# Two attention merges on GpSimd, one maximum for two lists, and a row scaling two steps later

## The chip, the core and the metric

The kernel runs on one core of a Trainium2 chip. A core has a matrix engine (TensorE, PE in the profile, with its weight loads as PEld), a vector engine (VectorE, DVE), an engine for functions (ScalarE, ACT), a general engine (GpSimd, POOL) and a queue that issues transfers (SyncE, SP). Each engine works through its own list of instructions in order and waits on semaphores for the others. The metric is the device time of one execution in microseconds; three runs of the kernel before took 1610.02 to 1610.79 us, with a median of 1610.67.

## What is computed

One decoder block over 1024 tokens of width 1024. Attention runs in three dilation groups with 8 heads each; the groups are merged per head with weights that come from their softmax denominators. Beside it runs a gated causal convolution. Both are mixed, normalised by rows and added to the input, and a SwiGLU feed-forward network follows. Cut to what the change touches:

```python
for g, (window, dilation) in enumerate(DILATED_GROUPS):
    o_g, lse_g = dilated_group_attention(q[:, :, g], k[:, :, g], v[:, :, g], tab, window, dilation)
alpha = softmax(stack(lses), axis=0)               # weights of the three groups
o = einsum('gbsh,gbshd->bshd', alpha, stack(outs)) # the merge
y_attn = o.reshape(B, S, 512) @ w_attn_out
...
x = x + rms_norm(merged @ w_mix_out, g_post_mix)
h = rms_norm(x, g_pre_ffn)                         # the row scaling
x = x + rms_norm(swiglu_ffn(h, w_ffn_in, w_ffn_out), g_post_ffn)
```

## The kernel before

Nearly all products are made of three 16-bit products each: a number is split into a high and a low half precision part after a scaling by a power of two, and high times high, high times low and low times high are added up. The scalings need bounds of the numbers' sizes; `largest` (L176) makes such a bound of one or two parameter vectors: ScalarE squares each list of 8 numbers per partition (L182), VectorE adds the second list to the first where there are two (L186) and takes the maximum (L187). One call has two lists (L264, the scale and offset of the convolution's normalisation); it falls into the stage of the gates, where TensorE runs quarter products (L619 to L621), VectorE the convolution (L1003) and GpSimd the weights' subtractions (L458, L477 and others). L1103 adds two quarter results on VectorE, and a later product waits for it.

The order of the work is written out by hand. TensorE's instructions are issued in a fixed sequence, and after every three 512-column products (six 256-column ones) `tick` (L363) counts a step and lets background generators issue a piece of work on the other engines. A generator that yields n is left alone for n steps: `yield 1` moves what follows two steps down, `yield 3` four. `later(n, ...)` plans a piece n steps ahead. So the changes in the kernel are changes of the engine and of the position in the engines' lists; what runs when is then settled by the semaphores.

Attention (L1283) goes over twelve pairs of a group and a pair of heads, eight blocks of 128 queries each. Of each block TensorE makes the scores (L1355), VectorE adds the bias and takes a minimum (L1359), ScalarE takes exponentials (L1369), TensorE transposes (L1392), ScalarE and VectorE split the result (L1397, L1405), and TensorE multiplies by the values (L1421 to L1423). The transposes come three blocks after the scores and the values five. The score banks, the transpose banks and the output banks in PSUM are two each. For the next pair GpSimd copies keys and queries to the other half of the partitions (L1207, L1208) and scales the bias tile (L1212), a few blocks ahead. GpSimd's queue also issues the stores of values (L1247), of statistics and outputs (L1378).

A pair's merge (L1437) begins when the third group of a pair of heads is done. `hp` is the pair of heads, 0 to 3; those of 0 and 1 fall between 700 and 755 us, in the middle of attention, those of 2 and 3 at its end. It loads the first two groups' outputs (L1222), makes the weights of the groups in small instructions on VectorE (L1452 to L1461), multiplies the three outputs by them (L1465, 128x1024 each), adds them (L1467, L1470), has ScalarE sum the squares (L1473), and has TensorE transpose the result (L1487). The results of hp 0 and 1 are stored (L1502) and loaded again later (L1510).

After attention the mixing product runs over row tiles of 128 tokens, the first two together, then one by one (L1944, 48 products a tile). Behind each tile a generator (L1639) works on its rows: sums of squares on ScalarE (L1624), a row factor and the residual on VectorE (L1632, L1636), then the second normalisation: ScalarE's sum of squares (L1647), a root and five small VectorE instructions for the row factor (L1606), and ScalarE's scaling of the rows by it (L1649). After tiles 3 and 7 the four scaled tiles are transposed in eight groups (L1657), three steps apart after tile 3 and two after tile 7; each group takes one of two PSUM banks, which ScalarE empties (L1663) before it splits the group (L1531, with VectorE's L1532). ScalarE also splits weights in that stage (L448).

Of the kernel before, what the change touches and what calls it, by code (L numbers as in the profile page):

```python
# [14 lines left out]
AF = mybir.ActivationFunctionType  # L15
OP = mybir.AluOpType
AX = mybir.AxisListType
# [54 lines left out]
class Build:  # L72
# [103 lines left out]
    def largest(self, k, *cols, after=0):  # L176

        nc = self.nc
        q = [self.tiny(8, "pq", 4) for _ in cols]
        m = self.tiny(1, "pm", 4)  # L180
        for x, c in zip(q, cols):
            nc.scalar.activation(x, self.col8(c), AF.Square, scale=k)  # L182

        def most():
            if len(q) > 1:
                nc.vector.tensor_tensor(q[0], q[0], q[1], op=OP.add)  # L186
            nc.vector.tensor_reduce(m, q[0], AX.X, OP.max)  # L187

        if after:
            self.later(after, most)  # L190
        else:
            most()
        return m
# [1243 lines left out]
    def merge(self, hp, st, last):  # L1437


        nc = self.nc  # L1440

        late = 1 + (hp > 1)
        while hp > 1 and hp > len(self.OT) + 2:
            yield 0
        O = [*self.others(hp), last]
        last = None
        yield 1 + late
        t = self.tiny(96, "mrg", 2)
        m, r = (t[:, i * 16:(i + 1) * 16].rearrange("p (u e) -> p u e", u=8) for i in range(2))
        w = t[:, 48:].rearrange("p (g u e) -> p g u e", g=3, u=8)  # L1450
        low, tot = st[:, :, :, 0:2], st[:, :, :, 2:4]
        nc.vector.tensor_reduce(m, low.rearrange("p g u e -> p u e g"), AX.X, OP.min)  # L1452
        nc.vector.tensor_tensor(w, low, m.unsqueeze(1).to_broadcast([128, 3, 8, 2]), op=OP.subtract)
        nc.scalar.activation(t[:, 48:], t[:, 48:], AF.Exp, scale=-1.0)
        yield late
        nc.vector.tensor_tensor(tot, tot, w, op=OP.mult)
        nc.vector.tensor_reduce(m, tot.rearrange("p g u e -> p u e g"), AX.X, OP.add)
        nc.vector.reciprocal(r, m)
        x = t[:, 16:32]
        nc.vector.tensor_scalar(x, x, self.vun, None, op0=OP.mult)  # L1460
        nc.vector.tensor_tensor(w, w, r.unsqueeze(1).to_broadcast([128, 3, 8, 2]), op=OP.mult)  # L1461
        for g in range(3):
            y = O[g].rearrange("p (u h c) -> p u h c", u=8, h=2)
            a = w[:, g].unsqueeze(3).to_broadcast([128, 8, 2, 64])
            nc.vector.tensor_tensor(y, y, a, op=OP.mult)  # L1465
            yield late
        nc.vector.tensor_tensor(O[1], O[1], O[2], op=OP.add)  # L1467
        O[2] = y = a = None
        yield late
        nc.vector.tensor_tensor(O[0], O[0], O[1], op=OP.add)  # L1470
        O[1] = None
        yield 2
        nc.scalar.activation(self.junk, O[0], AF.Square, scale=self.o_scale, accum_out=self.osq[:, hp:hp + 1])  # L1473
        self.measured += 1
        if hp == 3:
            assert self.measured == 4
            self.mixing = self.bg(self.mix_scales())
        yield 1 + 2 * late
        if hp < 2:
            hi = self.slot()  # L1480
        else:
            hi, lo = self.two(T)
        for h in range(2):
            ps = self.bank("t")
            r = slice(h * 64, h * 64 + 64)
            for u in range(8):
                nc.tensor.transpose(ps.rearrange("p (m u) -> p u m", u=8)[:, u], O[0][r, u * 128:(u + 1) * 128],  # L1487
                                    self.ident[r, r])
            y = ps
            a = hi[:, h * H:(h + 1) * H]  # L1490
            if hp > 1:
                nc.scalar.activation(a, y, AF.Copy, scale=self.o_scale)
                nc.vector.scalar_tensor_tensor(lo[:, h * H:(h + 1) * H], y, self.o_scale, a,
                                               op0=OP.mult, op1=OP.subtract)
            else:
                nc.scalar.copy(a, y)
            ps = y = a = None
            yield late
        if hp > 1:
            self.OT[hp] = hi, lo  # L1500
        else:
            self.nc.gpsimd.dma_start(self.d_ot[hp], hi)  # L1502
# [136 lines left out]
    def mix_norm(self, tt, banks, x):  # L1639
        nc = self.nc  # L1640
        x2 = self.ring()
        yield from self.residual(banks, x, self.g_mix, x2)
        nc.sync.dma_start(self.d_x2[tt], x2)
        yield 1
        hn = self.slot()
        ss = self.tiny(4, "ss", 4)
        nc.scalar.activation(hn, x2, AF.Square, scale=ROOT, accum_out=ss[:, 0:1])  # L1647
        r = self.rstd_rows(ss[:, 0:1], self.eps_rms)
        nc.scalar.activation(hn, x2, AF.Copy, scale=r)  # L1649
        self.hn[tt // 4].append(hn)  # L1650
        if tt % 4 == 3:
            yield 14 if tt == 3 else 8
            op, y = [], None
            for kt in range(8):
                ps = self.bank("s")
                for i in range(4):
                    nc.tensor.transpose(ps[:, i * 128:(i + 1) * 128], self.hn[tt // 4][i][:, kt * 128:(kt + 1) * 128], self.ident)  # L1657
                if y is not None:
                    op.append(self.split(y, H, F16))
                if kt % 2 == 0:  # L1660
                    x = self.slot()
                y = x[:, (kt % 2) * H:(kt % 2 + 1) * H]
                nc.scalar.activation(y, ps, AF.Copy, scale=self.gain[1][:, kt:kt + 1])  # L1663
                self.h2f[tt // 4].append(y)
                yield 2 if tt == 3 else 1
            op.append(self.split(y, H, F16))
            self.h2[tt // 4] = op
            self.hn[tt // 4] = None
# [723 lines left out]
```

## Time and profile before

| | before |
|---|---|
| median of 3 runs | 1610.67 us |
| the profiled execution | 1611.6 us |
| its span, first to last instruction | 1609.7 us |
| mean granted clock of TensorE | 0.997 |
| ScalarE busy | 1084.6 us |
| GpSimd busy | 451.6 us |

The page of the profile shows how long each engine was busy; a list of waits shows which instruction waited for which; a list by stretches shows the busy time of PE, PEld, DVE, ACT and POOL in that order, each with its count of instructions, then the granted clock, the share of the transfer engines and GB/s. In lists in order of time the columns are the start, the duration, the engine, the line of the kernel, the operation, what it writes and reads, its shape and how many; in brackets the idle time before it and what ended it. Lists of one line's instructions give the shortest, median and longest duration in ns. Matmul records overlap: one of 512 columns is shown with 0.38 us, and the next starts 0.22 us after it. In the table's profiled execution the clock of TensorE was at half in two stretches of 3.41 us in the middle of the run and at the very end, and else full.

### The profile page before, as it was taken

The numbers are of one execution on the slowest core, as the hardware profiler recorded it, in microseconds if no ns is written. First come the engines' busy times: TensorE is split into PE (matmuls) and PEld (weight loads), VectorE is DVE, ScalarE is ACT, GpSimd is POOL, SyncE is SP. The second block draws the span as 40 slices with busy tenths as digits, with TensorE's granted clock in tenths as the row PEclk, the third lists the DMA queues.
The fourth block names the chain that finished last, engine by engine and source line by source line (L and its number), as shares of the span: only waits on it lengthen the run. The fifth ranks groups of instructions, "written<-read, shape, count | busy, mean of one in ns | idle before, by whom it ended". The sixth has DMA issues, their size and how long they took to land.

```text
span 1609.7 us, 25675 instructions
## 1 busy us (share of the span) xinstructions
PE 1582.1 (98%) x9085; PEld 849.2 (53%) x9085; DVE 1265.0 (79%) x2458; ACT 1084.6 (67%) x2069; POOL 451.6 (28%) x377
## 2 busy tenths in 40 slices
PE   8999999999999999999999999999999999999998
PEld 7744444444444789976654444444444444444443
DVE  6889999988888878887686765876666666777887
ACT  6476678777787569877654747767666666465654
POOL 0006777777777253663502200000000000000000
PEclk9999999999999999999999999999999999999999
DMA  4353355555566865677848332044444334494424
GB/s 176 109 200 115 113 208 184 194 190 187 161 174 167 249 190 156 166 222 205 246 179 322 153 107 103 27 170 151 150 167 148 125 125 144 144 384 134 156 92 164
DMA packets 164381, 271.87 MB, mean 169 GB/s; under 512 B 63921, under 2 KB 83052, under 8 KB 164252
## 3 DMA queue, kind: packets, MB, share of 16 engines
q1 hardware_dynamic: 160044, 258.06, 47.9%
q0 software_dynamic: 3920, 11.91, 2.5%
q8 instruction: 71, 1.16, 0.3%
q14 instruction: 58, 0.48, 0.1%
q10 hardware_dynamic: 288, 0.27, 0.0%
HBM read 196.35 MB, written 78.55 MB: 171 GB/s over the span
## 4 chain that ended last, share of the span: by engine, by line
PE 78%; DVE 12%; ACT 5%; issue 2%; DMA 2%; POOL 0%; SPq 0%; DVEq 0%; ACTq 0%; POOLq 0%
PE p L619 14%; PE p L620 14%; PE p L621 14%; PE p L2274 9%; PE p L603 4%; PE p L607 4%; PE p L605 4%; DVE p L1003 2%; PE p L857 2%; PE p L1260 2%; PE p L1262 2%; PE p L1264 2%; PE p L1392 2%; DVE b L449 2%; PE p L1355 2%
## 5 line engine op out<-in xcount | busy, mean ns | idle before, releaser
L621 PE MATMUL p<-b,b 128*128 128x512 f16 x1032 | 391.1, 379 | 1.4 <-POOL b L458 1.4
L620 PE MATMUL p<-b,b 128*128 128x512 f16 x1032 | 391.0, 379 | 0.0
L619 PE MATMUL p<-b,b 128*128 128x512 f16 x1032 | 391.0, 379 | 0.1
L2274 PE MATMUL p<-b 128*128 128x512 f16 x924 | 199.9, 379 | 0.6 <-DVE b L449 0.5
L621 PEld LDWEIGHTS <-b 128*128 128x128 f16 x1032 | 100.9, 98 | 124.6 <-POOL b L458 3.3
L619 PEld LDWEIGHTS <-b 128*128 128x128 f16 x1032 | 101.0, 98 | 121.0
L1003 DVE SCALAR_TENSOR_TENSOR p<-b,par,p 128x511 f32<-128x511 f32 (+14 forms) x232 | 164.1, 739 | 0.0
L620 PEld LDWEIGHTS <-b 128*128 128x128 f16 x1032 | 100.8, 98 | 116.8 <-issue 0.3
L2274 PEld LDWEIGHTS <-b 128*128 128x128 f16 x924 | 90.4, 98 | 110.0 <-issue 1.4
L603 PE MATMUL p<-b,b 128*128 128x512 f16 (+1 forms) x368 | 140.8, 383 | 1.6 <-ACT b L448 1.6
L607 PE MATMUL p<-b,b 128*128 128x512 f16 (+1 forms) x368 | 140.6, 382 | 0.4 <-DVE b L449 0.4
L605 PE MATMUL p<-b,b 128*128 128x512 f16 (+1 forms) x368 | 140.2, 381 | 0.0
L458 POOL TENSOR_TENSOR b<-d,b 128x1024 f16<-128x1024 f32 x44 | 93.9, 2133 | 89.9 <-ACT b L457 89.9
L449 DVE SCALAR_TENSOR_TENSOR b<-d,sc,b 128x1024 f16<-128x1024 f32 x40 | 51.3, 1282 | 85.9 <-ACT b L448 85.9
L1260 PE MATMUL p<-b,b 128*128 128x256 f16 x384 | 104.7, 273 | 0.1
L1264 PE MATMUL p<-b,b 128*128 128x256 f16 x384 | 104.7, 273 | 0.0
L1262 PE MATMUL p<-b,b 128*128 128x256 f16 x384 | 104.7, 273 | 0.0
L1369 ACT ACTIVATE c<-c,stat 128x128 f32<-128x128 f32 (+1 forms) x192 | 84.4, 444 | 6.2 <-DVE stat L1359 6.1
L1944 PE MATMUL p<-b,b 128*128 128x512 f16 x384 | 85.8, 383 | 0.0
L1359 DVE CUSTOM_DVE_ANT_0 c<-p,bt,sig 128x128 f32<-128x128 f32 (+1 forms) x192 | 70.7, 406 | 16.2 <-PE p L1355 11.6
L1003 DVE SCALAR_TENSOR_TENSOR p<-c,pairs,p 128x511 f32<-128x511 f32 (+6 forms) x112 | 82.7, 739 | 0.0
L449 DVE SCALAR_TENSOR_TENSOR b<-c,fs,b 128x512 f16<-128x512 f32 x77 | 57.4, 745 | 24.6 <-ACT b L448 24.5
(352 smaller groups left out, 3480.1 us busy)
## 6 DMA issues: line engine op xcount, KB each, us to landing
b<-w_in SPq DMA_DIRECT2D x30, 512.0 KB, 4.7
b<-w_v SPq DMA_DIRECT2D x24, 512.0 KB, 4.6
b<-w_fi SPq DMA_DIRECT2D x24, 512.0 KB, 6.2
d<-w_in SPq DMA_DIRECT2D x23, 512.0 KB, 4.2
dqS<-c SPq DMA_DIRECT2D x44, 256.0 KB, 2.2
b<-w_fo SPq DMA_DIRECT2D x22, 512.0 KB, 4.3
b<-w_fo SPq DMA_DIRECT2D x44, 256.0 KB, 5.4
c<-dqS SPq DMA_DIRECT2D x44, 256.0 KB, 4.1
```

The source lines that it names most:

```text
L449: self.nc.vector.scalar_tensor_tensor(lo, x, w, hi, op0=OP.mult, op1=OP.subtract)
L603: nc.tensor.matmul(ps, hi[:, s], a, start=kt == 0, stop=False)
L605: nc.tensor.matmul(ps, hi[:, s], b, start=False, stop=False)
L607: nc.tensor.matmul(ps, lo[:, s], a, start=False, stop=kt == nk - 1)
L619: nc.tensor.matmul(ps, hi[:, s], a, start=first and kt == 0, stop=False, skip_group_check=True)
L620: nc.tensor.matmul(ps, hi[:, s], b, start=False, stop=False, skip_group_check=True)
L621: nc.tensor.matmul(ps, lo[:, s], a, start=False, stop=kt == 3, skip_group_check=True)
L1003: nc.vector.scalar_tensor_tensor(A[i][:, j:], src[i][:, :H - j], w[i], A[i][:, j:], op0=OP.mult, op1=OP.add)
L1260: nc.tensor.matmul(o, a, hi[:, s], start=kt == 0, stop=False)
L1262: nc.tensor.matmul(o, a, lo[:, s], start=False, stop=False)
L1264: nc.tensor.matmul(o, b, hi[:, s], start=False, stop=kt == KT - 1)
L2274: nc.tensor.matmul(acc[t], x, y, start=first and e == 0, stop=last and e == 2, skip_group_check=True)
```

## The change

Three things are changed. `largest` puts the squares of its one or two lists side by side in one tile of 16 and takes a single maximum of all of them, instead of adding the lists first. In the merges of hp 0 and 1 the three products and two sums are issued to GpSimd instead of VectorE, with four steps between them instead of two, and six steps instead of three to the sum of squares; the merges of hp 2 and 3 stay on VectorE at their places. In `mix_norm` the scaling of the rows comes two steps after the row factor instead of in the same one.

```diff
     def largest(self, k, *cols, after=0):
...
-        q = [self.tiny(8, "pq", 4) for _ in cols]
+        q = self.tiny(16, "pq", 4)
         m = self.tiny(1, "pm", 4)
-        for x, c in zip(q, cols):
-            nc.scalar.activation(x, self.col8(c), AF.Square, scale=k)
+        for i, c in enumerate(cols):
+            nc.scalar.activation(q[:, 8 * i:8 * i + 8], self.col8(c), AF.Square, scale=k)
 
         def most():
-            if len(q) > 1:
-                nc.vector.tensor_tensor(q[0], q[0], q[1], op=OP.add)
-            nc.vector.tensor_reduce(m, q[0], AX.X, OP.max)
+            nc.vector.tensor_reduce(m, q[:, :8 * len(cols)], AX.X, OP.max)
...
         late = 1 + (hp > 1)
+        by, gap = (nc.gpsimd, 3) if hp < 2 else (nc.vector, late)
...
         for g in range(3):
             y = O[g].rearrange("p (u h c) -> p u h c", u=8, h=2)
             a = w[:, g].unsqueeze(3).to_broadcast([128, 8, 2, 64])
-            nc.vector.tensor_tensor(y, y, a, op=OP.mult)
-            yield late
-        nc.vector.tensor_tensor(O[1], O[1], O[2], op=OP.add)
+            by.tensor_tensor(y, y, a, op=OP.mult)
+            yield gap
+        by.tensor_tensor(O[1], O[1], O[2], op=OP.add)
         O[2] = y = a = None
-        yield late
-        nc.vector.tensor_tensor(O[0], O[0], O[1], op=OP.add)
+        yield gap
+        by.tensor_tensor(O[0], O[0], O[1], op=OP.add)
         O[1] = None
-        yield 2
+        yield 5 if hp < 2 else 2
         nc.scalar.activation(self.junk, O[0], AF.Square, scale=self.o_scale, accum_out=self.osq[:, hp:hp + 1])
...
         nc.scalar.activation(hn, x2, AF.Square, scale=ROOT, accum_out=ss[:, 0:1])
         r = self.rstd_rows(ss[:, 0:1], self.eps_rms)
+        yield 1
         nc.scalar.activation(hn, x2, AF.Copy, scale=r)
```

## The prediction

> **What bounds the kernel now.** I read the page first, then who TensorE waited for (over the whole run, then from 700 to 735 us), then the stretches around the longest waits with the granted clock.
>
> ```profile
> span 1609.7 us, 25675 instructions
> PE 1582.1 (98%) x9085; PEld 849.2 (53%) x9085; DVE 1265.0 (79%) x2458; ACT 1084.6 (67%) x2069; POOL 451.6 (28%) x377
> ...
> PE p L1657 <- ACT b L1663: 3.7, 2, 2.9
> PE p L619 <- DVE c L1103: 2.3, 1, 2.3
> ```
> ```profile
> PE p L1392 <- DVE c L1405: 0.8, 1, 0.8
> PE p L1487 <- DVE c L1405: 0.8, 1, 0.8
> PE p L1355 <- DVE stat L1359: 0.5, 2, 0.3
> ```
> ```profile
> 706.00:722.00 16.00, 14.66 (x143) 10.86 (x142) 15.50 (x40) 10.96 (x35) 5.00 (x7) 1.00 0.73 220
> 720.53:723.95 3.42, 1.91 (x16) 1.07 (x14) 3.14 (x10) 2.87 (x9) 2.57 (x4) 1.00 0.34 101
> 723.95:727.36 3.41, 3.36 (x20) 2.15 (x20) 3.24 (x11) 1.73 (x6) 0.00 (x0) 0.50 0.27 77
> ...
> 966.29:969.71 3.42, 1.11 (x7) 0.78 (x8) 1.87 (x3) 3.42 (x7) 0.00 (x0) 1.00 0.28 105
> 969.71:973.12 3.41, 3.41 (x11) 1.78 (x10) 2.34 (x5) 3.41 (x8) 0.00 (x0) 0.50 0.00 0
> ```
>
> TensorE sets the time: 1582 of 1610 us. Only stalls of TensorE can be won, and a relieved engine gains nothing by itself. Three stalls lie where the change has a part: one wait of 2.3 us (L619), a group of short ones between 706 and 727, and one of 2.9 us in the transposes of L1657. After the last two the clock stands at 0.50 for 3.41 us; each such stretch follows one in which TensorE was busy 1.91 or 1.11 of 3.42 us. The stages between these places run without waits, so what is won there should reach the end.
>
> **One maximum.** L186, the sum of two lists of 8 numbers, goes; L187 reduces 16 numbers instead of 8.
>
> ```profile
> 202.34 1.99 DVE L186 TENSOR_TENSOR pq<-pq,pq 128x8 f32<-128x8 f32 x1
> ...
> 205.72 0.15 DVE L187 TENSOR_REDUCE pm<-pq 128x1 f32<-128x8 f32 x1
> 205.79 0.73 DVE L1003 SCALAR_TENSOR_TENSOR p<-b,par,p 128x500 f32<-128x500 f32 x1
> ```
> ```profile
> 202.18 2.12 POOL L458 TENSOR_TENSOR b<-d,b 128x1024 f16<-128x1024 f32 x1 [1.11 <-ACT b L457]
> ...
> 205.61 1.27 POOL L478 TENSOR_TENSOR d<-d,d 128x512 f32<-128x512 f32 x1
> ```
> ```profile
> 204.54 0.38 PE L621 MATMUL p<-b,b 128*128 128x512 f16 x1
> 207.18 0.38 PE L619 MATMUL p<-b,c 128*128 128x512 f16 x1 [2.26 <-DVE c L1103]
> ```
>
> L186 took 1.99 us for 8 elements and ended with POOL's L458 (202.18 + 2.12): it stood still while POOL worked. The two instructions beside POOL's L478 did not: L187 reads one list, L1003 one operand from SBUF and one from PSUM. So VectorE is 2.0 us earlier at L1103, for which TensorE waits. TensorE starts a 512-column matmul every 0.22 us, so L619 would have begun at 204.76 and lost 2.4 us; 0.4 of it stays, **2.0 us go**.
>
> **The merges on GpSimd.** Per merge five VectorE instructions go; GpSimd gets them, the first product at the old step, each next one four steps later instead of two.
>
> ```profile
> L1465 DVE TENSOR_TENSOR b<-b,mrg x12: 1212/1218/1226, 706.2 to 839.6; 128x1024 f32<-128x1024 f32 x12
> L1025 POOL TENSOR_TENSOR b<-b,b x7: 2357/2367/2380, 226.8 to 530.0; 128x1024 f32<-128x1024 f32 x7
> L1212 POOL TENSOR_SCALAR bt<-bt,rsig x12: 1562/1563/2595, 570.4 to 802.9; 128x512 f32<-128x512 f32 x12
> ```
> ```profile
> 705.64 0.50 DVE L1461 TENSOR_TENSOR mrg<-mrg 128x48 f32<-128x48 f32 x1
> ...
> 728.77 0.35 DVE L1359 CUSTOM_DVE_ANT_0 c<-p,bt,sig 128x128 f32<-128x128 f32 x1 [0.99 <-issue]
> ```
> ```profile
> 703.46 0.61 POOL L1207 COPY b<-b 64x512 f16<-64x512 f16 x1
> ...
> 707.22 1.62 POOL L1212 TENSOR_SCALAR bt<-bt,rsig 128x512 f32<-128x512 f32 x1 [1.14 <-DMA bt<-rep]
> ```
> ```profile
> 719.02 1.15 ACT L1473 ACTIVATE junk<-b,cs 128x1024 bf16<-128x1024 f32 x1
> ```
>
> VectorE is freed of 5 x 1.22 = 6.1 us, once around 706 to 717 and once around 726 to 738. In the first of these it was busy 15.50 of 16 us; that is why TensorE waited for L1359 and L1405. What TensorE lost there: waits of 0.5 + 0.8 + 0.8 = 2.1 us; 0.16 more for each of about five gaps, since a record lasts 0.38 and the next matmul could start after 0.22: 0.8; and half of the 2.6 us at half clock that aren't waited through (3.41 less 0.8): 1.3. Together 4.2. Around the second merge no wait is listed, so its 6.1 us buy nothing.
>
> GpSimd's price for a product with a broadcast factor isn't in the trace. Bounds: 2.37 us, the plain sum of the same size (L1025), and 3.1 us, twice the 512 elements of L1212. I take 2.4, the nearer form. Queued behind the products on POOL are the four copies and the bias scaling for the next group of heads (L1207, L1212, done by 708.8 so far), a store of v, more copies and the stores of statistics. With the factors ready at 706.1: three products to 713.3, four copies (2.6) to 715.9, bias to 717.5. VectorE needs that bias first at 728.77, some 5 us earlier once the stalls are gone, so there are about 6 us to spare; at 3.1 us still 4. The v store (1.6), a sum, four copies and the other sum end near 726.5; L1473, on ScalarE with the softmax queued behind it, stood 11 steps and 12.8 us after the first product and now stands 22 steps after it, near 729 without the stalls. No wait is added for ScalarE or for the transposes 4 steps on. The second merge has its last sum after the next group's copies and comes within about 1 us of its L1473; softmax results are used two rounds later, so I cost that at 0, at 1 us if that cover fails. The stores of both results come later on POOL's queue, still some 40 steps before SP loads them.
>
> A cost comes from the contention seen at L186, which a large sum on POOL has too:
>
> ```profile
> 530.01 2.36 POOL L1025 TENSOR_TENSOR b<-b,b 128x1024 f32<-128x1024 f32 x1 [2.20 <-DVE b L1013]
> ```
> ```profile
> 530.73 2.18 DVE L449 SCALAR_TENSOR_TENSOR b<-b,es,b 128x512 f16<-128x512 f32 x1 [0.20 <-ACT b L448]
> ```
>
> L449 reads two operands from SBUF and took 2.18 us: 1.64 until the sum ended at 532.37, and 0.54 after it. During the three products VectorE has only L1359, L1405 and L1273, which read PSUM. The first sum meets the second merge's small instructions (L1453) and perhaps one L449: one block of 1.2 to 2 us. A round of attention lasts over 2 us here and two banks of scores are kept, so most of it is covered: I charge 0.4, bounds 0 and 2. **4.2 - 0.4 = 3.8 us go.**
>
> By the Trainium skill, page "SBUF — State Buffer", section "Who interferes with whom", a VectorE instruction with two SBUF inputs contends with a GpSimd instruction that reads SBUF, and the later one blocks entirely; the trace agrees (1.99 and 2.18 us above). By this rule each of the ten new instructions can hold VectorE's two-input ones for its whole length, which is the first rival below.
>
> **Rows scaled later.** L1649 moves two steps down for all eight row tiles; the transposes that follow tiles 3 and 7 move with it.
>
> ```profile
> 934.37 1.15 ACT L1649 ACTIVATE b<-d,rr 128x1024 f32<-128x1024 f32 x1 [0.87 <-DVE rr L1616]
> ...
> 937.75 1.15 ACT L1649 ACTIVATE b<-d,rr 128x1024 f32<-128x1024 f32 x1 [0.86 <-DVE rr L1616]
> 938.81 0.67 ACT L1624 ACTIVATE d<-p,cs 128x512 f32<-128x512 f32 x1
> ...
> 963.34 1.06 ACT L1647 ACTIVATE b<-d 128x1024 f32<-128x1024 f32 x1 [2.63 <-DVE d L1636]
> ...
> 965.69 1.15 ACT L1649 ACTIVATE b<-d,rr 128x1024 f32<-128x1024 f32 x1 [0.87 <-DVE rr L1616]
> ...
> 967.86 0.68 ACT L1663 ACTIVATE b<-p,hg 128x512 f32<-128x512 f32 x1
> ...
> 969.56 0.69 ACT L1663 ACTIVATE b<-p,hg 128x512 f32<-128x512 f32 x1
> ```
> ```profile
> 962.95 2.75 PE L1944 MATMUL p<-b,b 128*128 128x512 f16 x12
> 968.60 0.66 PE L1657 MATMUL p<-ident,b 128*128 128x128 f32 x4 [2.89 <-ACT b L1663]
> ...
> 980.29 1.03 PE L1944 MATMUL p<-b,b 128*128 128x512 f16 x4
> ```
>
> ScalarE idles 0.87 us before every L1649, until VectorE has the row factor. Tiles 0 and 1 run in the same steps: with L1649 later, tile 1's L1647 fills tile 0's wait and the reverse, and L1624 of tile 2 starts 1.8 us before 938.81. From there the chain L1624, VectorE, L1647, L1649 follows itself, so tile 4's L1647 starts at 961.5 instead of 963.34. Behind it now comes the first L1663 (its transposes are two steps, 1.3 us, later), ahead of L1649: L1647 with its accumulator and root to 962.9, L448 0.6, L1663 to 964.1. TensorE reaches the third transposes, which need that bank, at 963.8. So it waits 0.3 us instead of 2.9, and from there ScalarE's 1.7 us per group (967.86 to 969.56) is under TensorE's mean 2.4 (1.95 of matmuls, 0.44 of transposes). Without stalls, TensorE's 48 matmuls and five groups of transposes from 962.95 take 48 x 0.216 + 5 x 0.44 = 12.6 us; it needed 17.3, to 980.29. The 4.7 lost hold the half-clock stretch. Less 0.3, **4.4 us go**. If the gain on tiles 0 and 1 didn't carry, L1663 would end at 965.9 and the wait be 2 us: 2.7 gained, the lower bound, 1.2 less if the half clock comes too. Tile 7's moved transposes have ScalarE's next work before them instead of behind; I cost that at 0, bounds -1 and 1.
>
> By the Trainium skill, page "TensorE: Matmul & The Clock Gate", section "What's actually happening", the clock halves after an idle window of 3413 ns on a free-running raster; the two stretches of 3.41 us agree. By it a wait of 2 us could still cost a half-clock stretch, which is in the second rival.
>
> **Sum.** 2.0 + 3.8 + 4.4 = 10.2 us off the profiled run. That run took 1611.6 us (its span 1609.7 and 1.9 around it), 0.9 over the median of 1610.67. So 1611.6 - 10.2 = 1601.4 there, a span near 1599.5, and **1600.5** as a median.
>
> **The rivals.** (1) *GpSimd's instructions hold VectorE.* For it: L186 and L449, both held to the end of a POOL instruction. Against: nothing of that kind is due during the products. It would leave 0 to 1.5 us of the merge's 3.8: 1602.8 to 1604.3. (2) *The transposes' wait moves on instead of going*, with the clock still halving: the 4.4 shrink to 0 to 1.5, 1603.4 to 1604.9. For it: ScalarE is busy 3.42 of 3.42 us there. (3) *Both*, with only the 2.0 left, or the rows' move undone by tile 7: 1607.5 to 1610. (4) *Slower: POOL's queue becomes the bound.* If the broadcast product takes X us, the bias is ready at 710.3 + 3X, and VectorE, then TensorE, wait for it from X = 4.5 on, 3 us for each further us. With the merge's 3.8 lost as well, the kernel is slower than before from X = 6.6; at X = 8 it loses 3 x 3.5 = 10.5 against 6.4 won, 1614.8. Against it: the medians of POOL's rows above stay under 3.1 ns per element of a partition, 3.2 us for 1024.
>
> **How the numbers follow.** Chances: forecast 0.55 (1598 to 1603), rival 1 0.17, rival 2 0.14, rival 3 0.08, rival 4 0.06. The lower end, 1598, takes all of 2.4 + 4.2 + 4.7 and 1 us at tile 7; the upper, 1606, takes in rivals 1 and 2. What a measurement of this kernel can tell from no change is about 0.2%, 3.2 us. Faster than 1607.4: 0.86; within: 0.08; slower: 0.06.
>
> **What would show it.** Right: no L186, L619 no longer waiting 2.3 us for L1103; no wait for L1359 or L1405 between 700 and 735, ten POOL products and sums of about 2.4 us, the granted clock at 1.00 throughout; L1657 waiting under 1 us for L1663. Wrong: POOL's L1212 as a releaser of L1359; L449 or L1453 at 2 us beside a POOL sum with TensorE waiting behind it; a half-clock stretch left around 965; products over 3.1 us.

## The result and the profile after

| | before | after |
|---|---|---|
| median, 7 runs each in turn | 1610.74 us | 1606.0 us (1603.24 to 1606.55) |
| ratio | | 0.9963 [0.9953, 0.9973] |
| profiled execution | 1611.6 us | 1606.55 us |
| its span | 1609.7 us | 1604.8 us |

The changed kernel is faster by 4.7 us, about half of the 10.2 forecast; the time lies at the very end of the range, 1606. How long each engine was busy, from the page of its profile, and TensorE's waits (who waited for whom: us in total, times, longest):

```profile
PE 1580.5 (98%) x9085; PEld 848.1 (53%) x9085; DVE 1257.4 (78%) x2447; ACT 1083.7 (68%) x2069; POOL 471.4 (29%) x387
```
```profile
PE p L1657 <- ACT b L1663: 2.5, 1, 2.5
...
PE p L1390 <- DVE c L1403: 1.0, 1, 1.0
...
PE p L1486 <- DVE c L1403: 0.5, 1, 0.5
...
PE p L617 <- DVE c L1101: 0.4, 2, 0.3
PE p L1657 <- ACT b L1649: 0.2, 1, 0.2
```

The lines of the kernel have moved: L1465 is now L1464, L1467 is L1466, L1470 is L1469, L1473 is L1472, L1405 is L1403, L449 is L447, L619 is L617 and L1103 is L1101; L1649 to L2031 stay. Of the 2.3 us wait for L1101, 0.3 is left, and the waits for VectorE's bias (L1357) are gone. One wait of L1390 for L1403 remains, and L1657 still waits 2.5 us for L1663, but at another place. The stretches show where:

```profile
706.00:722.00 16.00, 16.00 (x162) 12.18 (x161) 13.74 (x42) 11.64 (x36) 15.32 (x16) 1.00 0.62 185
...
961.00:965.00 4.00, 4.00 (x24) 2.41 (x23) 2.86 (x5) 4.00 (x9) 0.00 (x0) 1.00 0.00 1
965.00:969.00 4.00, 4.00 (x22) 1.95 (x20) 3.29 (x10) 3.97 (x9) 0.00 (x0) 1.00 0.00 0
```
```profile
997.10:1000.60 3.50, 1.28 (x7) 0.49 (x5) 1.26 (x5) 2.67 (x5) 0.00 (x0) 1.00 0.37 144
1000.60:1004.00 3.40, 3.14 (x10) 1.70 (x11) 0.92 (x2) 2.81 (x5) 0.00 (x0) 0.51 0.00 0
```

From 706 to 722 TensorE is busy all the time, VectorE 13.74 instead of 15.50 us. The transposes behind tile 3, where the old kernel stalled at 966 to 969, run here from 958 on, and the stretches from 961 to 969 are full at full clock. The half clock has gone from 724 and from 970; there is a new stretch of it at 1000.6, behind a new stall: in tile 7's transposes.

To size the terms, the start of one and the same product of TensorE is compared in two traces; where the gap between the two grows, the stage in between has won. By this the terms of the changed kernel's profiled run are (us won):

| stage (us of before) | forecast | changed kernel |
|---|---|---|
| one maximum (204 to 212) | +2.0 | +2.0 |
| merges (704 to 770) | +3.8 | +2.7 |
| rows later, mix stage (957 to 1000) | +4.4 | +4.5 |
| tile 7 (1000 to 1100) | 0 | -3.95 |
| all else | 0 | -0.2 |
| whole run | 10.2 | 5.0 |

Two terms are right within 0.1 us, one is 1.1 short, and one that was costed at nothing took 4.

**The merges.** In order of time, first GpSimd and VectorE, then TensorE and ScalarE:

```profile
704.25 5.62 POOL L1464 TENSOR_TENSOR b<-b,mrg 128x1024 f32<-128x1024 f32 x3 [2.57 <-DVE mrg L1460]
...
715.77 2.37 POOL L1466 TENSOR_TENSOR b<-b,b 128x1024 f32<-128x1024 f32 x1
...
721.26 2.38 POOL L1469 TENSOR_TENSOR b<-b,b 128x1024 f32<-128x1024 f32 x1
```
```profile
715.68 3.02 DVE L447 SCALAR_TENSOR_TENSOR b<-b,es,b 128x512 f16<-128x512 f32 x1
...
722.01 1.67 DVE L1459 TENSOR_SCALAR mrg<-mrg,vun 128x16 f32<-128x16 f32 x1
...
748.03 1.95 DVE L447 SCALAR_TENSOR_TENSOR b<-b,es,b 128x512 f16<-128x512 f32 x1 [1.27 <-ACT b L446]
```
```profile
724.57 0.66 PE L1390 MATMUL p<-ident,c 128*128 128x128 f32 x4 [0.97 <-DVE c L1403]
```
```profile
749.46 1.15 ACT L1472 ACTIVATE junk<-b,cs 128x1024 bf16<-128x1024 f32 x1 [1.47 <-POOL b L1469]
```

The products are cheaper than thought: 5.62 us for three, 1.87 each. But both sums of the first merge hold VectorE. L447 takes 3.02 us and ends at 718.70, 0.56 after the sum (715.77 + 2.37 = 718.14); L1459, 16 numbers per partition, takes 1.67 us and ends at 723.68, just after the second sum (723.64). TensorE pays for it at 724.57. In the second merge the last sum comes late: it holds L447 for 1.95 us, and ScalarE waits 1.47 us for it.

**Tile 7.** ScalarE, before and then after, and two rows of TensorE for each:

```profile
1002.19 1.15 ACT L1649 ACTIVATE b<-d,rr 128x1024 f32<-128x1024 f32 x1 [0.87 <-DVE rr L1616]
1003.35 1.28 ACT L2030 ACT_TABLE_LOAD   x1
1004.65 0.69 ACT L2030 ACTIVATE c<-p,sc 128x512 f32<-128x512 f32 x1
1005.23 0.68 ACT L1663 ACTIVATE b<-p,hg 128x512 f32<-128x512 f32 x1
1006.15 0.63 ACT L1974 ACTIVATE junk<-c 128x512 bf16<-128x512 f32 x1 [0.24 <-DVE c L2031]
```
```profile
1007.06 0.17 PE L157 MATMUL p<-pb,ones 128*128 128x1 bf16 x1
1008.02 0.65 PE L1657 MATMUL p<-ident,b 128*128 128x128 f32 x4 [0.80 <-ACT b L1663]
```
```profile
995.55 1.15 ACT L1649 ACTIVATE b<-d,rr 128x1024 f32<-128x1024 f32 x1 [0.87 <-DVE rr L1615]
996.71 1.28 ACT L2030 ACT_TABLE_LOAD   x1
998.01 0.69 ACT L2030 ACTIVATE c<-p,sc 128x512 f32<-128x512 f32 x1
999.51 0.63 ACT L1974 ACTIVATE junk<-c 128x512 bf16<-128x512 f32 x1 [0.82 <-DVE c L2031]
...
1000.14 0.67 ACT L1663 ACTIVATE b<-p,hg 128x512 f32<-128x512 f32 x1
```
```profile
998.21 0.17 PE L157 MATMUL p<-pb,ones 128*128 128x1 bf16 x1
1000.86 1.12 PE L1657 MATMUL p<-ident,b 128*128 128x128 f32 x4 [2.49 <-ACT b L1663]
```

Two things can be read here. The first L1663 now stands behind L1974, and so behind VectorE's L2031 (0.82 us of waiting): the order on ScalarE has changed. And the same matmul of L157 is 1007.06 - 998.21 = 8.85 us earlier than before, but L1649 only 1002.19 - 995.55 = 6.64: the rows' work has fallen 2.2 us behind TensorE. Which of the two makes the loss can't be read from one trace. **Theory I:** the order. **Rival II:** tile 7's rows come late in any order.

### The profile page after: what moved, and what is told of

It is laid out like the page before. It is cut to its first block, busy times and chain, and to the rows that moved or that the text cites. A ratio compares the mean times of both kernels' runs of the same rounds, so it can differ in the third digit from the quotient of the medians.

```text
span 1604.8 us, 25680 instructions
## 1 busy us (share of the span) xinstructions
PE 1580.5 (98%) x9085; PEld 848.1 (53%) x9085; DVE 1257.4 (78%) x2447; ACT 1083.7 (68%) x2069; POOL 471.4 (29%) x387
## 4 chain that ended last, share of the span: by engine, by line
PE 74%; DVE 14%; ACT 6%; issue 3%; DMA 2%; POOL 1%; SPq 0%; DVEq 0%; ACTq 0%; POOLq 0%
PE p L617 13%; PE p L619 13%; PE p L618 13%; PE p L2274 9%; PE p L601 3%; PE p L603 3%; PE p L605 3%; DVE p L1001 3%; PE p L855 2%; PE p L1258 2%; PE p L1260 2%; PE p L1262 2%; DVE b L447 2%; PE p L1353 2%; PE p L1390 2%
## 5 line engine op out<-in xcount | busy, mean ns | idle before, releaser
L619 PE MATMUL p<-b,b 128*128 128x512 f16 x1032 | 391.1, 379 | 1.3 <-POOL b L456 1.3
L617 PE MATMUL p<-b,b 128*128 128x512 f16 x1032 | 391.0, 379 | 0.0
L619 PEld LDWEIGHTS <-b 128*128 128x128 f16 x1032 | 100.9, 98 | 124.9 <-POOL b L456 3.6
L617 PEld LDWEIGHTS <-b 128*128 128x128 f16 x1032 | 101.0, 98 | 120.7
L447 DVE SCALAR_TENSOR_TENSOR b<-d,sc,b 128x1024 f16<-128x1024 f32 x40 | 51.3, 1282 | 87.0 <-ACT b L446 87.0
L1357 DVE CUSTOM_DVE_ANT_0 c<-p,bt,sig 128x128 f32<-128x128 f32 (+1 forms) x192 | 70.7, 406 | 17.7 <-PE p L1353 14.6
L447 DVE SCALAR_TENSOR_TENSOR b<-c,fs,b 128x512 f16<-128x512 f32 x77 | 57.3, 745 | 24.7 <-ACT b L446 24.6
```

The source lines that it names most:

```text
L447: self.nc.vector.scalar_tensor_tensor(lo, x, w, hi, op0=OP.mult, op1=OP.subtract)
L617: nc.tensor.matmul(ps, hi[:, s], a, start=first and kt == 0, stop=False, skip_group_check=True)
L619: nc.tensor.matmul(ps, lo[:, s], a, start=False, stop=kt == 3, skip_group_check=True)
```

## The experiments

Every kernel was timed in turn with the kernel before on the same chip. The gains by stage are worked out as above, from each kernel's own trace against that of before.

| kernel | median, us | before there | ratio [interval] | merges | mix | tile 7 |
|---|---|---|---|---|---|---|
| rows later alone | 1610.07 | 1611.24 | 0.9992 [0.9983, 1.0001] | 0 | +4.5 | -2.4 |
| merges alone | 1609.54 | 1611.24 | 0.9989 [0.9980, 0.9998] | +2.7 | +0.35 | -0.35 |
| square later | 1603.32 | 1611.24 | 0.9952 [0.9938, 0.9966] | +2.7 | +4.5 | -1.65 |
| Silu later | 1604.03 | 1611.24 | 0.9955 [0.9943, 0.9968] | +2.7 | +4.5 | -1.9 |
| tile 7 as before | 1604.13 | 1610.92 | 0.9958 [0.9945, 0.9970] | +2.7 | +4.5 | -2.3 |
| sums on VectorE | 1601.67 | 1610.92 | 0.9943 [0.9930, 0.9955] | +4.8 | +4.5 | -1.6 |
| first merge only | 1605.99 | 1610.92 | 0.9970 [0.9959, 0.9981] | +1.0 | +4.5 | -1.6 |
| early table load | 1603.21 | 1610.92 | 0.9952 [0.9939, 0.9964] | +2.7 | +4.5 | -1.1 |
| sums and table | 1601.17 | 1610.55 | 0.9942 [0.9928, 0.9956] | +4.8 | +4.5 | -1.1 |
| changed kernel again | 1604.64 | 1610.55 | 0.9962 [0.9950, 0.9975] | +2.7 | +4.5 | -2.4 |

The maximum is worth 2.0 us in the eight that have it and 0.0 in the first two. Within 0.1 us the terms of the maximum, the merges and the mix stage are the same wherever the same edit stands, so they add; tile 7's depends on the order there and on the clock. Starts of execution and waits elsewhere differ by up to 1.4 us from trace to trace; the stage columns are free of that, the medians are not.

**Rows later alone** (the kernel before with this one line):

```diff
         r = self.rstd_rows(ss[:, 0:1], self.eps_rms)
+        yield 1
         nc.scalar.activation(hn, x2, AF.Copy, scale=r)
```

> The kernel before with the rows scaled two steps later and nothing else. Theory I (the move wins in the mix stage and is given back at tile 7, because ScalarE's first L1663 falls behind the table load, the Silu and a square there): +4.5 us around 965, -3.8 near 1001, so 1610.0 us (1608.5 to 1611), with TensorE waiting 2.0 to 2.7 us in the first transposes of L1657 near 1003 and a half-clock stretch there. Forecast's sum: 4.4 less, 1606.3, with no wait over 0.5 us near 1003.

The time is that of theory I, 1610.07, but the trace is so only in part: TensorE waits 2.5 us for L1663 near 1003 as expected, yet no half-clock stretch follows, and tile 7 loses 2.4 instead of 3.8. That makes a gain of 2.1 by the stages; by the medians it is 1.2, in an interval that includes none, and this trace lost 0.6 where nothing was changed. That the rows' move alone is worth 4.4 is refuted.

**Merges alone** (the kernel before with the change's `merge`):

> The kernel before with the merges of hp 0 and 1 on GpSimd and nothing else. Theory I (VectorE is held by the sums and the sum of squares waits for GpSimd): 2.7 less, 1608.0 us (1607 to 1609), one VectorE instruction of L449 with two SBUF operands at 2 to 3 us beside a sum, and L1473 waiting over 1 us for POOL. Forecast's sum: 3.8 less, 1606.9. If the merges had been the whole loss: 1610 or more.

The stage gives +2.7, as in the changed kernel, with an L449 of 3.02 us and L1474 (L1473 above) waiting 1.5 us for POOL; the median is 1.5 above theory I's value and outside its 1607 to 1609. The profiled run lost 1.2 us between 212 and 704, where nothing was changed; whether the others did isn't shown. The stage column says that the merges fell 1.1 short of the forecast's 3.8, with or without the other edits.

**Square later** (the changed kernel; the first half tile's square L1974 moves behind L1663):

```diff
-        B.later(3 - j * hf, lambda: measure(2 * j + hf + 1, o))
+        B.later(3 - j * hf if j or hf else 18, lambda: measure(2 * j + hf + 1, o))
```

> The changed kernel with the square of the first half tile of the feed-forward product (L1974) planned 18 steps later instead of 3, so that ScalarE's first L1663 of tile 7 stands right behind the Silu. Theory I (order on ScalarE makes the stall): the wait of L1657 for L1663 goes from 2.5 to about 1.1 us and the half-clock stretch after it goes too: 2.5 to 3 less, about 1603.3 us (1602.5 to 1604.5). Rival II (ScalarE and VectorE reach tile 7's end no earlier than before, so that TensorE waits there in any order): 1605.5 to 1606.5, the wait stays above 2 us or comes back within 10 us.

1603.32 us, a wait of 0.9 us, no half clock: as theory I had it. But tile 7 still loses 1.65.

**Silu later** (the changed kernel; table load, Silu and its product behind the first L1663 too):

```diff
+        def tail():
+            if first:
+                nc.scalar.activation(o, gate, AF.Silu, scale=B.scale[fi[j][0]][1])
+            nc.vector.scalar_tensor_tensor(o, ps, B.scale[fi[j][1]][1], o, op0=OP.mult, op1=OP.mult)
...
+        if first:
+            B.later(5, tail)
...
-        B.later(3 - j * hf, lambda: measure(2 * j + hf + 1, o))
+        B.later(18 if first else 3 - j * hf, lambda: measure(2 * j + hf + 1, o))
```

> The changed kernel with the first half tile's Silu and its product (with the table load before it) planned 5 steps later and its square 18 later, so that the first L1663 of tile 7 comes ahead of the table load. Theory I: no wait over 0.5 us in L1657 near 1001 and no half-clock stretch there, 3.8 to 4.2 less: about 1601.9 us (1601 to 1603.5). Rival II (ScalarE and VectorE are late there in any order): 1605 to 1606.5, with a wait of over 1.5 us in L1657 or in the products behind it.

1604.03, between the two. L1657 no longer waits for L1663, yet 1.9 us are lost in pieces of 0.3 to 0.8, the first for VectorE (L160, queued behind the late product). Theory I's 1601.9 fails: putting L1663 first only moves the loss. The loss in any order that rival II foretold is there, but without its wait of over 1.5 us and without the half clock that its number held.

**Tile 7 as before** (the changed kernel with `if tt != 7:` ahead of the added `yield 1`):

> The changed kernel with the rows of tile 7 scaled in their old step; tiles 0 to 6 as in the change. Theory I (only the order on ScalarE was wrong): L1663 is ahead of the table load again, the 2.5 us wait and the half-clock stretch at 1001 go, 3.8 less than the changed kernel's 1606.0: 1602.2 us (1601.5 to 1603). Rival II (the row factor of tile 7 comes no earlier than in the changed kernel, so transposes two steps earlier wait for L1649 instead): a wait of L1657 for L1649 of about 2 us in place of 0.2, 1604.2 us, or 1605.8 with a half-clock stretch after it.

```profile
PE p L1658 <- ACT b L1650: 1.5, 1, 1.5
...
PE p L1658 <- ACT b L1664: 1.3, 1, 1.3
```

In TensorE's waits of this kernel (one line lower than above) the wait for L1650, the scaling of tile 7's rows, is 1.5 us where the changed kernel had 0.2, and L1664 is waited for another 1.3 us, where the kernel before had 0.8. Rival II's 1604.2, measured 1604.13. The old order doesn't bring back the old ease. On ScalarE:

```profile
995.20 1.15 ACT L1650 ACTIVATE b<-d,rr 128x1024 f32<-128x1024 f32 x1 [0.87 <-DVE rr L1615]
```

The scaling of tile 7's rows starts 1002.19 - 995.20 = 7.0 us earlier than before, TensorE is 9.2 us ahead of before there, and the difference of 2.2 is what is lost (2.3).

Why the rows fall behind can be read one tile earlier. ScalarE and VectorE at tile 6's row work, before:

```profile
984.98 0.62 ACT L1531 CAST b<-b 128x512 f16<-128x512 f32 x1
985.51 0.68 ACT L1624 ACTIVATE d<-p,cs 128x512 f32<-128x512 f32 x1
```
```profile
986.31 0.15 DVE L1626 TENSOR_SCALAR ss<-ss 128x1 f32<-128x1 f32 x1
```

The same in the changed kernel, where these lines are L1530, L1623, L1531 (VectorE's part of the split) and L1625:

```profile
977.53 0.68 ACT L1623 ACTIVATE d<-p,cs 128x512 f32<-128x512 f32 x1
...
978.85 0.62 ACT L1530 CAST b<-b 128x512 f16<-128x512 f32 x1
```
```profile
979.50 0.69 DVE L1531 TENSOR_TENSOR b<-b,b 128x512 f16<-128x512 f32 x1 [1.74 <-ACT b L1530]
980.11 0.15 DVE L1625 TENSOR_SCALAR ss<-ss 128x1 f32<-128x1 f32 x1
```

The row work of tile 6 starts 985.51 - 977.53 = 8.0 us earlier. But the split of the last transposed group of tile 3 now stands behind it on ScalarE, VectorE waits 1.74 us for that split, and the next step of the row work, L1625, is queued behind it: it starts only 6.2 us earlier, and at the scaling of tiles 6 and 7 the row work is 6.6 us ahead. In the last tile L1623 starts at 987.75, right behind tile 6's scaling and 4.7 us after TensorE has gone on to the next product (983.07); before it was 994.38 and 2.4 us. So the chain of row work sets when tile 7's rows are ready, not TensorE, and 1.4 of its 2.2 us of lag arise at this one place. With the rows' move alone it is the same: the row work has gained 3.6 us before this place and 2.2 after it. Whether another order there would win the 1.4 was not tried.

**Sums on VectorE** (square later, and the two sums of each early merge back on VectorE):

```diff
-        by.tensor_tensor(O[1], O[1], O[2], op=OP.add)
+        nc.vector.tensor_tensor(O[1], O[1], O[2], op=OP.add)
...
-        by.tensor_tensor(O[0], O[0], O[1], op=OP.add)
+        nc.vector.tensor_tensor(O[0], O[0], O[1], op=OP.add)
```

> The kernel with the square planned 18 steps later (1603.3 us), and the two sums of each merge of hp 0 and 1 back on VectorE; the six products stay on GpSimd. If GpSimd's sums hold VectorE's instructions: no L447 over 1.3 us and no L1459 over 0.5 us between 712 and 750, the wait of L1390 for L1403 (1.0 us) and the sum of squares' wait for POOL go, 1602.0 us (1601.3 to 1602.8). If VectorE's load and not the holding makes that wait (2.4 us of work come back to it per merge): the wait stays or grows, 1603 to 1605.

One line's instructions between 700 and 760 us (count; shortest, median and longest in ns), L447 in the changed kernel:

```profile
L447 DVE SCALAR_TENSOR_TENSOR b<-b,es,b x6: 750/956/3019, 713.1 to 748.0; 128x512 f16<-128x512 f32 x6
```

L447, and L1459 over the whole run, in this kernel:

```profile
L447 DVE SCALAR_TENSOR_TENSOR b<-b,es,b x6: 735/745/785, 713.8 to 747.5; 128x512 f16<-128x512 f32 x6
```
```profile
L1459 DVE TENSOR_SCALAR mrg<-mrg,vun x4: 234/234/235, 704.2 to 829.7; 128x16 f32<-128x16 f32 x4
```

The holds are gone, between 700 and 760 us no wait of TensorE is listed any more, ScalarE no longer waits for POOL, and the merges are worth 4.8 instead of 2.7, although VectorE has 2.4 us more to do in each. So the sums on GpSimd cost 2.1 us of TensorE's time, by holding and by coming late; VectorE's load was not it.

**First merge only** (square later; the change's `by`, `gap` and last `yield` for hp 0 alone):

> The kernel with the square planned 18 steps later (1603.3 us), and only the merge of hp 0 on GpSimd, that of hp 1 on VectorE in its old steps. Theory I (the second merge on GpSimd wins nothing and costs the 2.4 us that TensorE loses from 755 to 770, behind a sum of squares that waits for POOL): 1.5 to 2.4 less, 1601.4 us (1600.8 to 1602.3), with no wait of L1472 for POOL. Rival (VectorE can't carry the second merge around 726 to 738 either): 1603 to 1605, with waits of L1353 or L1390 for VectorE there.

A miss for theory I, and above the rival's 1603 to 1605 as well, though the wait of L1390 that the rival named is there: 1605.99. The second merge on GpSimd is worth 2.7 - 1.0 = 1.7 us. VectorE and TensorE in order of time:

```profile
722.26 1.67 DVE L1459 TENSOR_SCALAR mrg<-mrg,vun 128x16 f32<-128x16 f32 x1
723.96 0.21 DVE L1460 TENSOR_TENSOR mrg<-mrg 128x48 f32<-128x48 f32 x1
724.20 1.23 DVE L1464 TENSOR_TENSOR b<-b,mrg 128x1024 f32<-128x1024 f32 x1
725.35 0.68 DVE L1403 SCALAR_TENSOR_TENSOR c<-p,c 128x512 f16<-128x512 f32 x1
```
```profile
726.09 0.66 PE L1390 MATMUL p<-ident,c 128*128 128x128 f32 x4 [2.23 <-DVE c L1403]
```

The second merge's product on VectorE stands right behind the held L1459 and in front of L1403. Of the 2.4 us that I had called a loss between 755 and 770, 1.5 are none: the kernel with the sums on VectorE shows them as well, without a wait, since two groups of the merge's transposes (L1486, 0.75 us each) stand later in TensorE's list than before. Only 0.9 are waits.

**Early table load** (square later, and one Silu of a single column behind the row factor of tile 7, its result not used):

```diff
         r = self.rstd_rows(ss[:, 0:1], self.eps_rms)
+        if tt == 7:
+            nc.scalar.activation(ss[:, 2:3], ss[:, 0:1], AF.Silu)
         yield 1
```

> The kernel with the square planned 18 steps later (1603.3 us), and one Silu of a single column in tile 7 right behind the root of the row factor, so that ScalarE's table load falls into its wait of 0.87 us for the row factor. If the table load stands in the path of L1663: L1663 starts 0.9 us earlier, the wait of L1657 for it (0.9 us) goes, L1657's wait for L1649 grows from 0.3 to 0.7: 1602.8 us (1602.4 to 1603.1). If TensorE then waits elsewhere within 10 us: 1603.2 to 1603.8.

In time order on ScalarE of this kernel:

```profile
994.48 1.28 ACT L1649 ACT_TABLE_LOAD   x1
...
997.49 0.67 ACT L1665 ACTIVATE b<-p,hg 128x512 f32<-128x512 f32 x1
```

The emptying (L1663, here L1665) starts 0.95 us earlier than with the square alone (998.44), and the wait for it is gone; that for the scaling (L1651 here) is 0.8 instead of 0.3. Tile 7 loses 1.1 instead of 1.65. The median doesn't show this: 1603.21 beside 1603.32 on another chip, just inside the 1603.2 to 1603.8 of the other case.

**Sums and table** together:

> The square 18 steps later, the two sums of each merge of hp 0 and 1 on VectorE, and the early Silu of one column, together. If the gains add: the 1601.7 us of the kernel with the sums on VectorE less 0 to 0.6 for the table load, 1601.3 us (1600.9 to 1601.8), no half-clock stretch before the end, and no L447 over 1.3 us between 712 and 750. If the early table load only moves TensorE's wait to L1649: 1601.7 to 1602.2.

1601.17 us, as expected if the gains add (1601.3), and the fastest of all, though its interval overlaps that of the sums alone. The stages add: 2.0 + 4.8 + 4.5 - 1.1 = 10.2. That this is the forecast's sum is chance: the kernel is another one and its terms are others.

**The changed kernel again:**

> The changed kernel unaltered, for its profile and its spread (1603.2 to 1606.6 us so far) beside the kernels above on one chip. If the half-clock stretch behind the stall at 1001 depends on where its 3.41 us fall and makes the spread: times in two groups about 1.6 us apart, and the profiled run's time in the upper group exactly when its profile shows the stretch. If the stretch always follows the stall: 1606.0 with it, 1605.5 to 1606.6 in nearly all runs.

Around the stall at 999 in this execution:

```profile
997.40:1000.80 3.40, 1.57 (x8) 0.68 (x8) 1.26 (x5) 2.57 (x5) 0.00 (x0) 1.00 0.51 200
1000.80:1004.20 3.40, 2.75 (x17) 1.82 (x18) 0.99 (x2) 3.27 (x6) 0.00 (x0) 1.00 0.00 0
```
```profile
1001.46 0.66 PE L1657 MATMUL p<-ident,b 128*128 128x128 f32 x4 [2.49 <-ACT b L1663]
```

The stall is the same 2.49 us, but the clock stays at 1.00, tile 7 loses 2.4 instead of 3.95, and the run took 1604.64 instead of 1606.55 us. The twelve runs of the changed kernel lie in two groups, seven from 1603.24 to 1604.69 and five from 1606.0 to 1606.59, none in between. With one profile in each group this supports the reading that the half clock, about 1.5 us, makes the groups; it is not settled for the ten runs without a profile. It means that the median of 1606.0 is that of the upper group, which had four of the seven.

## Why the prediction was right and wrong

The direction held, and the range held just: its upper end, 1606, was made for rivals 1 and 2, and what used it up was mostly tile 7, which had been given 1 us at most. That it held is luck. The forecast itself was 5.5 us too fast, by its own steps:

- **TensorE is the bound, and a stall won reaches the end: right for the maximum and the merges, wrong for the mix stage**, whose gain was mostly lost again at tile 7. Between the merges and the mix stage, from 770 to 957, the gap between the traces changes by 0.02 us at most in every trace.
- **One maximum, 2.0: right**, 2.0 in the nine traces that have it, 0.0 in the two without it.
- **Rows later, 4.4 in the mix stage: right**, 4.5 in all ten traces that have it, with the half clock gone and TensorE busy 4.00 of 4 us around 967. Rival 2, the wait moving on inside that stage, did not come.
- **Tile 7 at 0, bounds -1 and 1: this step failed.** It was put as "Tile 7's moved transposes have ScalarE's next work before them instead of behind; I cost that at 0, bounds -1 and 1". The sentence names the place, but I looked at the order alone. It is -2.4 with the clock full and -3.95 with the half clock. The reason is mainly one that the order at tile 7 doesn't touch: the edit makes TensorE 4.5 us earlier and the row work of the last tile only some 2.2, so in the old order TensorE loses 2.3 there as well, at L1650 and L1664. The working had the numbers for this: by it tile 4's L1647 starts 1.8 us earlier (measured 6.4 - 4.4 = 2.0), and "From there the chain L1624, VectorE, L1647, L1649 follows itself", while TensorE gains 4.4; the difference was not carried on to tile 7. Better orders saved 0.75 (square later) and 1.3 (with the table load ahead), and with them no half clock was seen. The forecast's own rival 3 held "the rows' move undone by tile 7", at 0.08; it came about by half with the clock full and almost wholly with the half clock, and alone the move kept 1.2 us by the medians, 2.1 by the stages. Rival 3's 1607.5 to 1610 was no price for that: without the 4.4 alone the sum gives 1600.5 + 4.4 = 1604.9.
- **The 4.2 that TensorE lost at the merges: right in kind, short in size**; with the sums on VectorE, and so without the holds, the stage gave 4.8.
- **0.4 for the holds, bounds 0 and 2: mis-sized.** The sums on GpSimd cost 2.1, with what their lateness adds. I had counted one block of 1.2 to 2 us and covered most of it by the two banks of scores. There were two long ones in the first merge, 3.02 and 1.67 us, and one of 1.95 in the second. The rule of the Trainium skill that made rival 1, page "SBUF — State Buffer", section "Who interferes with whom", also lists `tensor_scalar` among the instructions that can use the pair of ports shared with GpSimd; L1459 is one, its 1.67 us agree (0.23 unheld), and I had counted the second merge's small instructions into the one block. Rival 1 (1602.8 to 1604.3) thus came in part, in the sums and not in the products.
- **The second merge's last sum, "I cost that at 0, at 1 us if that cover fails": too little.** L1472 waits 1.47 us for L1469 there; in the first merge it doesn't wait, as forecast. The share of this isn't told apart from the holds'.
- **"Around the second merge no wait is listed, so its 6.1 us buy nothing": wrong.** They buy 1.7, beside a first merge whose sums hold VectorE. What they buy without these holds was not tried.
- **GpSimd's price, 2.4 taken, bounds 2.37 and 3.1: too high**, 1.87 a product. Rival 4, POOL's queue as the bound, was nowhere near.

Of the 5.15 us by which the profiled run missed its 1601.4, tile 7 has 3.95 and the merges 1.1.

## What to carry to other kernels

When a stall is taken away, ask at the end of that stage which engine's work is no earlier: the gain of TensorE is kept only as far as the chain that it meets next has moved too, and a comparison of how much earlier each of them starts shows it at once. Before work goes to GpSimd, list what VectorE issues during each of its instructions, the small ones as well; here the products could go for nothing and the sums cost more than they freed. A stall also costs what the clock does behind it, and that can differ from run to run.

## What the runs showed of the hardware

- GpSimd's products with a broadcast factor (1.87 us) are faster than its plain sums of the same size (2.37).
- VectorE's L447 is recorded from 715.68, 0.09 us before GpSimd's sum, and was still held until the sum was over. By the Trainium skill, page "SBUF — State Buffer", section "Who interferes with whom", the one that issues first has the pair of ports; the start of a record evidently doesn't tell which that was.
- The same stall of 2.49 us was followed by 3.41 us at half clock in one execution and not in another. In each trace the changes of the clock lie a whole number of windows of 3.413 us apart: 290 from 10.78 to 1000.65 us in the one, 465 from 10.56 to 1597.76 in the other. Counted on from there, most of the stall falls into one window in the first (997.24 to 1000.65, TensorE busy 1.14 us), and in the second it is split between two (997.01 to 1000.43, busy 1.69, and 1000.43 to 1003.84, busy 2.38). By the Trainium skill, page "TensorE: Matmul & The Clock Gate", section "What's actually happening", the window runs freely, so its place against the stall may differ; the two traces agree with that. The section speaks of an idle window; here TensorE was busy for 1.14 us of it.
- How little work halves the clock isn't settled by the busy time: in the kernel before, the window from 720.54 to 723.95 (busy 1.90 us) was followed by the half clock, and that from 205.12 to 208.54 (busy 1.36) was not.
